# Writing down the order of TensorE, ScalarE and VectorE in the experts of a transformer block

## The chip, the cores and the metric

The kernel runs on one core of a Trainium2 chip. A core has a matrix engine (TensorE, PE in the rows), two elementwise engines (VectorE, DVE, and ScalarE, ACT), GpSimd (POOL) and SyncE (SP), which here issues most DMAs. Each engine takes its own instructions in the order in which they stand in its queue; semaphores hold one back until what it needs is there. The metric is the device time of one execution in microseconds, as the median of several runs.

## The reference

Two transformer layers on 256 tokens of width 1024. The second layer ends in a mixture of eight experts, and only that part is touched here:

```
logits = jnp.dot(t, w_router)                       # t: 256 x 1024
top_val, top_idx = lax.top_k(logits, 2)             # two experts for each token
gates = softmax(top_val) spread over the 8 experts
hid = silu(t @ e_w1) * (t @ e_w3)                   # e_w1, e_w3: 1024 x 3584 for each expert
y = sum over experts of (hid @ e_w2) * gate         # e_w2: 3584 x 1024
```

All inputs are float32; the weights of the experts alone are 352 MB.

## The kernel before

**Work of a chunk.** The tokens of an expert (at most 128) are gathered into one tile of 128 rows. Its 3584 hidden columns are taken in seven chunks of 512, so there are 56 chunks (`for e`, `for i`). For each chunk TensorE multiplies the tokens by w1 (into PSUM bank `b1`, 5 or 3) and by w3 (bank `b3`, 6 or 4). ScalarE takes silu of `b1` into the tile `nat` (L587), VectorE multiplies it by `b3` (L588). Four transposes on TensorE turn `nat` (`hid_t`, L599), and the turned tile is multiplied by w2 into banks 0 and 1, `y` (`down`). The down matmuls of a chunk are issued one chunk later (`pend`), behind the next chunk's w1 and w3.

**Splits.** float32 is reached by splitting every operand into a high and a low float32r part: ScalarE writes the high part `wh` (L154), VectorE the difference `wl` (L155). A product takes three matmuls (`mm3`): high by high (L176), high by `wl` (L177), low by `wh` (L178). One split covers 1024 columns of weights, two products of 512, so six matmuls. A chunk has twelve splits: four for w1, four for w3, four for w2. I number them 0 to 11. The pool `split` has four buffers of `wh` and four of `wl`, so ScalarE can split at most four splits ahead of TensorE. The turned hidden tile is split the same way (L182 high, L183 low, both named `ol_t`), as are the turned tokens of the next expert (`turn_x`, L876, split into `oh_t`).

**Weights.** SyncE loads 1 MB tiles (`raw`) into a ring of sixteen buffers in four pools; `load_ahead` issues a load as soon as, in program order, a buffer of the ring is used up.

**Order.** A scheduler places the instructions of each engine by its own estimate of when they are ready; `behind(a, b)` pins `a` behind `b` on one engine. In the experts before the change only a few places are pinned (the end of the routing, the gate product behind `added`).

**Sums at the end.** Seven experts send their result to DRAM (`store_y`); in the last expert `fetch` clears two ring buffers on GpSimd and gathers each token's rows into them, and `add_rows` adds them to `ht`, two VectorE instructions for each half of the tokens (L847).

Of the kernel before, what the change touches and what calls it, by code (L numbers as in the profile page):

```python
# [3 lines left out]

# [21 lines left out]
NE = 8  # L26
# [19 lines left out]
def block_kernel(ctx: ExitStack, tc: tile.TileContext, x, w_qkv, w_o, mixer_norm, ffn_norm,  # L46
# [91 lines left out]
    def stream(n, g=None, hold=(None, None), free=2):  # L138


        got = taken = 0
        while got < n:
            load_ahead()
            t = loaded[n_used[0]]
            _, nk, fn = jobs[n_used[0]]
            n_used[0] += 1
            k = min(nk, HALF // fn)
            for c0 in range(0, nk, k):
                wh = split.tile([P, HALF], F32R, name="wh")
# [24 lines left out]

    def mm3(ps, s, m, start, stop):
        i0 = nc.tensor.matmul(ps, s[0], m[0], start=start, stop=False)  # L176
        nc.tensor.matmul(ps, s[0], m[1], start=False, stop=False)  # L177
        i1 = nc.tensor.matmul(ps, s[1], m[0], start=False, stop=stop)  # L178
        return i0, i1

    def split_out(src, h, l):
        return (nc.scalar.activation(h, src, AF.Copy),  # L182
                nc.vector.tensor_sub(l, src, h.bitcast(F32)))  # L183
# [408 lines left out]
                                           op1=ALU.mult)  # L592
        return t

    def hid_t(t, n, ps, a, c, apart=True):
        k = n // P
        tv = t[:, :n].rearrange("p (f j) -> p j f" if apart else "p (j f) -> p j f", j=k)
        for j in range(k):
            nc.tensor.transpose(ps[:, j * P:(j + 1) * P], tv[:, j], ident)  # L599
        split_out(ps[:, :n], a[:, :n], c[:, :n])  # L600
        return [(a[:, j * P:(j + 1) * P], c[:, j * P:(j + 1) * P]) for j in range(k)]

    def down(ps, hT, j, w, start, stop):
        for half in range(2):
            mm3(ps[half], hT[j], tuple(a[:, half * FC:(half + 1) * FC] for a in w),
                start and j == 0, stop and j == len(hT) - 1)

    def dense_ffn(pool, hold, then):
        y = [[bank[0], bank[1]], [bank[2], bank[7]]]
# [2 lines left out]
        for i, (f0, n) in enumerate(fcs):  # L612
            if i == 0:
                for k in range(2):
                    ws = list(stream(NC, 2, hold[0]) if k == 0 else stream(NC, 2, hold[1], 0))
                    for b in range(NB):
                        for c, w in enumerate(ws):
# [2 lines left out]
                hid = [gate_mul(pool.tile([P, FC], F32, name="hid"), bank[3 + 2 * b],  # L620
                                bank[4 + 2 * b], n, rms[2][b]) for b in range(NB)]
                hT = [hid_t(hid[b], n, y[b][0], pool.tile([P, FC], F32R, name="hth"),
                            pool.tile([P, FC], F32R, name="htl"), False) for b in range(NB)]
            else:
                for k in range(2):
                    for c, w in enumerate(stream(NC, 2)):
# [215 lines left out]
                bounds_check=(NE - 1) * P - 1, oob_is_err=False)  # L842
        return t

    def add_rows(b, t):
        for k in range(2):
            i0 = nc.vector.scalar_tensor_tensor(ht[b], t[:, k * D:(k + 1) * D],  # L847
                                                ex[:, 1 + k, b:b + 1], ht[b], op0=ALU.mult,
                                                op1=ALU.add)
        return i0  # L850
# [5 lines left out]

    def store_y(e):
        t = ep.tile([P, D], F32, name="yr")
        nc.scalar.activation(t[:, :FC], y[0], AF.Copy)
        nc.vector.tensor_copy(t[:, FC:], y[1])  # L860
        nc.gpsimd.dma_start(ys_d[e * P:(e + 1) * P], t)


    def mark(e, b):
        return nc.vector.tensor_scalar(pe[:, b], iota, slot[:, b, e:e + 1], None, op0=ALU.is_equal)

    def take(i, bk):
        split_out(bank[bk], eh[:, 4 * i:4 * i + 4].rearrange("p c t -> p (c t)"),
                  el[:, 4 * i:4 * i + 4].rearrange("p c t -> p (c t)"))

    def turn_x(t, banks, later):

        for i in range(2):
            for c in range(4):
                cc = 4 * i + c
                behind((nc.tensor.transpose(bank[banks[i]][:, c * P:(c + 1) * P],  # L876
                                            t[:, cc * P:(cc + 1) * P], ident), later))
            take(i, banks[i])

    def gather(banks, later):  # L880

# [51 lines left out]
                i1 = nc.vector.tensor_add(ht[b][:, hs], ht[b][:, hs], ps)  # L933
        return i0, i1

    pend, done, added = None, None, None
    gather((3, 4), raws[2])
    k = 0
    most_v = None
# [2 lines left out]
    for e in range(NE):  # L942
        for i, (f0, n) in enumerate(ecs):
            b1, b3 = (5, 6) if k % 2 == 0 else (3, 4)
            k += 1
            for bk in (b1, b3):
# [12 lines left out]
            pend = (i, t, b1)  # L959
            if i == 0:  # L960
                if e:
                    store_y(e - 1)
                else:
                    gates()
                    send()
# [22 lines left out]
    hT = hid_t(pend[1], FC, bank[pend[2]], *(sp[0][:, i * FC:(i + 1) * FC] for i in range(2)))  # L988

    row = ep.tile([P, FC], F32, name="nat")  # L990
    one = sp[0][:, D:D + P]
# [142 lines left out]
```

## Time and profile before

| | |
|---|---|
| median of 3 runs | 1439.82 us (1438.69 to 1440.4) |
| profiled execution | 1438.46 us, of which 1436.8 us are the span from the first to the last instruction |
| TensorE busy | 1417.6 us, 99% |
| VectorE, ScalarE busy | 1170.2 us, 1010.3 us |
| mean granted TensorE clock | 0.996 of 2.4 GHz |
| DMA | 442 MB, 308 GB/s over the span |

The span is about 445 us of attention, dense layer and routing, then 966 us of experts (up to 1412 us), and 25 us of ending. Busy times are unions of intervals; a matmul's end is modelled, so TensorE reads as busy also where its matmuls start late. A stretch is therefore judged by how long the same work takes in it, not by its busy share.

### The profile page before, as it was taken

The page shows a single profiled execution, that of the slowest core. Times are in us where ns is not written, and L with a number is a line of the kernel's source. Part 1 is how long each engine was busy: PE and PEld are TensorE (multiplying, and loading weights), DVE is VectorE, ACT ScalarE, POOL GpSimd, SP SyncE. Part 2 cuts the span into 40 slices and gives each one's busy share as a digit, 9 for nine tenths or more (in the row PEclk, how much of TensorE's full clock was granted, in tenths as well). Part 3 has the DMA queues.
Part 4 walks back from the last instruction along what each step waited for, and adds up shares of the span by engine and source line. Part 5 has one row for each costly group of instructions (what it writes and reads, how often), then busy time and mean ns, then how long its engine had stood idle before and what let it go on. Part 6 is the DMA issues. An engine that isn't in the chain of part 4 may idle for free. (4 is left out here: it accounts for less than half of the span.)

```text
span 1436.8 us, 19637 instructions
## 1 busy us (share of the span) xinstructions
PE 1417.6 (99%) x7285; PEld 1176.7 (82%) x7285; DVE 1170.2 (81%) x1384; ACT 1010.3 (70%) x1282; POOL 45.3 (3%) x71
## 2 busy tenths in 40 slices
PE   9999999999999999999999999999999999999997
PEld 7877999988877888888888888878878887887775
DVE  6656766667667999999999988888888888898887
ACT  6656655546655778878878777777777777777765
POOL 1000000000001000000000000000000000000200
PEclk9999999999999999999999999999999999999998
DMA  9633865556566999999999999999999999999850
GB/s 353 236 117 108 303 196 186 186 173 228 180 246 218 402 401 388 385 373 373 388 392 362 391 362 373 366 381 368 354 389 372 357 380 380 358 374 369 320 189 32
DMA packets 172153, 442.11 MB, mean 308 GB/s; under 512 B 7299, under 2 KB 9395, under 8 KB 157972
## 3 DMA queue, kind: packets, MB, share of 16 engines
q1 hardware_dynamic: 166852, 422.61, 80.6%
q0 software_dynamic: 5136, 18.18, 3.5%
q8 instruction: 59, 0.97, 0.3%
q14 instruction: 42, 0.34, 0.1%
q10 hardware_dynamic: 64, 0.02, 0.0%
HBM read 430.00 MB, written 11.03 MB: 307 GB/s over the span
## 5 line engine op out<-in xcount | busy, mean ns | idle before, releaser
L155 DVE TENSOR_TENSOR wl<-raw,wh 128x1024 fp32r<-128x1024 f32 x710 | 834.4, 1220 | 112.9 <-ACT wh L154 106.0
L154 ACT ACTIVATE wh<-raw 128x1024 fp32r<-128x1024 f32 x710 | 725.6, 1057 | 133.9 <-PE bank L178 97.7
L177 PE MATMUL bank<-wl,oh_t 128*128 128x512 f32 x968 | 382.9, 396 | 2.9 <-DVE wl L155 2.0
L176 PE MATMUL bank<-wh,oh_t 128*128 128x512 f32 x968 | 375.5, 393 | 2.1 <-ACT wh L154 1.6
L178 PE MATMUL bank<-wh,oh_t 128*128 128x512 f32 x904 | 353.5, 391 | 0.1
L177 PEld LDWEIGHTS bank<-wl,oh_t 128*128 128x128 f32 x968 | 181.9, 188 | 60.0 <-DVE wl L155 18.9
L176 PEld LDWEIGHTS bank<-wh,oh_t 128*128 128x128 f32 x968 | 182.2, 188 | 41.4 <-ACT wh L154 1.8
L178 PEld LDWEIGHTS bank<-wh,oh_t 128*128 128x128 f32 x904 | 170.2, 188 | 34.1 <-DVE oh_t L183 0.8
L178 PE MATMUL bank<-wh,ol_t 128*128 128x512 f32 x504 | 194.6, 392 | 0.0
L162 ACT ACTIVATE wh<-raw,gcol 128x512 fp32r<-128x512 f32 (+1 forms) x192 | 123.8, 698 | 87.4 <-PE bank L318 56.3
L163 DVE SCALAR_TENSOR_TENSOR wl<-raw,gcol,wh 128x512 fp32r<-128x512 f32 (+1 forms) x192 | 131.1, 725 | 65.8 <-ACT wh L162 65.3
L177 PE MATMUL bank<-wl,ol_t 128*128 128x512 f32 x440 | 174.7, 397 | 0.4 <-DVE wl L155 0.4
L318 PE MATMUL bank<-x_h,wh 128*128 128x256 f32 x512 | 143.8, 282 | 0.0
L318 PE MATMUL bank<-x_h,wl 128*128 128x256 f32 x512 | 142.9, 280 | 0.0
L318 PE MATMUL bank<-x_l,wh 128*128 128x256 f32 x512 | 142.7, 279 | 0.0
L176 PE MATMUL bank<-wh,ol_t 128*128 128x512 f32 x440 | 137.1, 393 | 0.0
L178 PEld LDWEIGHTS bank<-wh,ol_t 128*128 128x128 f32 x504 | 94.4, 188 | 19.9 <-issue 1.1
L318 PEld LDWEIGHTS bank<-x_h,wh 128*128 128x128 f32 x512 | 95.9, 188 | 1.9 <-issue 1.1
L177 PEld LDWEIGHTS bank<-wl,ol_t 128*128 128x128 f32 x440 | 83.0, 189 | 16.4 <-DVE wl L155 0.6
L318 PEld LDWEIGHTS bank<-x_h,wl 128*128 128x128 f32 x512 | 96.1, 188 | 0.0
L318 PEld LDWEIGHTS bank<-x_l,wh 128*128 128x128 f32 x512 | 95.9, 187 | 0.2
L176 PEld LDWEIGHTS bank<-wh,ol_t 128*128 128x128 f32 x440 | 81.6, 188 | 16.8
(218 smaller groups left out, 1106.1 us busy)
## 6 DMA issues: line engine op xcount, KB each, us to landing
raw<-in_e_w_dram SPq DMA_DIRECT2D x335, 1024.0 KB, 7.3
raw<-in_w_dram SPq DMA_DIRECT2D x33, 1024.0 KB, 5.1
raw<-in_w_qkv_dram SPq DMA_DIRECT2D x22, 1024.0 KB, 5.7
raw<-in_w_o_dram SPq DMA_DIRECT2D x8, 1024.0 KB, 7.5
xs_d<-hn POOLq DMA_DIRECT2D x1, 4096.0 KB, 16.0
xr<-xs_d POOLq DMA_DIRECT2D x7, 512.0 KB, 7.5
ys_d<-yr POOLq DMA_DIRECT2D x7, 512.0 KB, 7.8
raw<-in_w_qkv_dram SPq DMA_DIRECT2D x4, 512.0 KB, 6.8
```

The lines of the kernel that those rows point to most:

```text
L154: i0 = nc.scalar.activation(wh[:, :m], src, AF.Copy)
L155: i1 = nc.vector.tensor_sub(wl[:, :m], src, wh[:, :m].bitcast(F32))
L162: i0 = nc.scalar.activation(wh[:, cs], src[:, cs], AF.Copy, scale=gc)
L163: i1 = nc.vector.scalar_tensor_tensor(wl[:, cs], src[:, cs], gc, wh[:, cs].bitcast(F32), op0=ALU.mult, op1=ALU.subtract)
L176: i0 = nc.tensor.matmul(ps, s[0], m[0], start=start, stop=False)
L177: nc.tensor.matmul(ps, s[0], m[1], start=False, stop=False)
L178: i1 = nc.tensor.matmul(ps, s[1], m[0], start=False, stop=stop)
L318: nc.tensor.matmul(to, w[a][:, ms], z[:, :, c], start=c + i + m % 2 == 0, stop=c == NC - 1 and m % 2 == 1 and i == 2, skip_group_check=True)
```

## The change

The instructions stay the same; only their order on the engines does not. Every matmul and transpose of the experts is now pinned behind the one before it in program order (`last`), so TensorE does w1, the four transposes, w3, then down, in every chunk. On ScalarE and VectorE each step that is not a weight split (`then`) stands behind the third split of the next weights, and the fourth split stands behind the step: the hidden tile's split and silu behind the third split of w3, the gate product and the next tokens' split behind the third split of w2, `store_y` behind the third split of the second chunk's w1. The fetch is issued one chunk earlier, and its four sums stand singly behind the third split of w1 in the last four chunks.

```diff
-    held, recent = [None, None], [None]
+    held, recent, lead = [None, None], [None, None], [None, None]
...
-                recent[0] = i0
+                recent[:] = i0, i1
...
+    def hid_t(t, n, ps, a, c, apart=True, after=None):
...
+            i0 = nc.tensor.transpose(ps[:, j * P:(j + 1) * P], tv[:, j], ident)
+            if after is not None:
+                behind((i0, after))
+                after = i0
+        h, l = split_out(ps[:, :n], a[:, :n], c[:, :n])
...
+    AHEAD, AHEAD_D = 6, 3
+
+    def ahead(ws, n):
+        return [next(ws) for _ in range(n)]
+
+    def then(act=None, dve=None):
+
+        for i, n in enumerate((act, dve)):
+            if n is not None:
+                behind((n, recent[i]), (n, lead[i]))
+                lead[i] = n
...
-                for c, w in enumerate(stream(NC, hold=held)):
-                    _, last = mm3(bank[bk], (eh[:, c], el[:, c]), w, c == 0, c == NC - 1)
-                if pend is not None and bk == b1:
-                    hT = hid_t(pend[1], FC, bank[pend[2]], *hts)
+                first = pend is None and bk == b1
+                ws = stream(NC, hold=held) if first else stream(NC, hold=lead, free=0)
+                got = [] if first else ahead(ws, AHEAD)
+                if bk == b1:
+                    if due is not None:
+                        then(*store_y(due))
+                        due = None
+                    if e == NE - 1 and i >= 3:
+                        then(dve=add_row((i - 3) // 2, (i - 3) % 2))
...
+                else:
+                    if pend is not None:
+                        hT, last, h, l = hid_t(pend[1], FC, bank[pend[2]], *hts, after=last)
+                        then(h, l)
+                    then(nc.scalar.activation(t[:, :n], bank[b1][:, :n], AF.Silu))
+                for c, w in enumerate(itertools.chain(got, ws)):
+                    i0, i1 = mm3(bank[bk], (eh[:, c], el[:, c]), w, c == 0, c == NC - 1)
+                    behind((i0, last))
+                    last = i1
+            if pend is not None:
+                ws = stream(4, hold=lead, free=0)
+                got = ahead(ws, AHEAD_D)
+            then(dve=nc.vector.tensor_mul(t[:, :n], t[:, :n], bank[b3][:, :n]))
             if i == len(ecs) - 1 and e + 1 < NE:
-                turn_x(xr, (2, 7), last)
-            t = gate_mul(ep.tile([P, FC], F32, name="nat"), bank[b1], bank[b3], n, after=added)
+                last = turn_x(xr, (2, 7), last)
             if pend is not None:
-                for j, w in enumerate(stream(4)):
-                    down(y, hT, j, w, pend[0] == 0, pend[0] == len(ecs) - 1)
+                for j, w in enumerate(itertools.chain(got, ws)):
+                    last = down(y, hT, j, w, pend[0] == 0, pend[0] == len(ecs) - 1, last)
...
-                elif i == 2:
+                elif i == 1:
                     came = [fetch(b) for b in range(NB)]
-                elif i in (4, 5):
-                    added = add_rows(i - 4, came[i - 4])
```

**Place 1: the hidden tile, middle experts.** On TensorE before, the four transposes (`nat` as input) that turn the hidden tile of the fourth expert's last chunk stand in the middle of the same chunk's down matmuls (banks 0 and 1), right after the product that makes `nat`:

```order
L177 MATMUL bank1_77<-wl_8574,ol_t_90 128x512
L178 MATMUL bank1_77<-wh_8573,ol_t_90 128x512
L599 MATMUL bank3_79<-ident_116,nat_8558 128x128 x4
L176 MATMUL bank0_76<-wh_8585,ol_t_90 128x512
L176 MATMUL bank1_77<-wh_8585,ol_t_90 128x512
L177 MATMUL bank0_76<-wl_8586,ol_t_90 128x512
```

The same transposes in the changed program, between the last w1 matmul (bank 5) and the first w3 matmul (bank 6) of the next chunk:

```order
L178 MATMUL bank5_81<-wl_8641,oh_t_89 128x512
L179 MATMUL bank5_81<-wh_8640,oh_t_89 128x512
L600 MATMUL bank3_79<-ident_116,nat_8452 128x128 x4
L177 MATMUL bank6_82<-wh_8652,oh_t_89 128x512
L178 MATMUL bank6_82<-wl_8653,oh_t_89 128x512
```

They moved back by 36 matmuls: twelve of down and the 24 of w1. On ScalarE in the same stretch before (`nat` is silu, `ol_t` the high part of the hidden tile):

```order
L154 ACTIVATE wh<-raw 128x1024 x8
L182 ACTIVATE ol_t<-bank_79 128x512
L154 ACTIVATE wh<-raw 128x1024 x4
L587 ACTIVATE nat<-bank_81 128x512
L154 ACTIVATE wh<-raw 128x1024 x8
```

and in the changed program:

```order
L155 ACTIVATE wh<-raw 128x1024 x12
L183 ACTIVATE ol_t<-bank_79 128x512
L988 ACTIVATE nat<-bank_81 128x512
L155 ACTIVATE wh<-raw 128x1024 x12
L183 ACTIVATE ol_t<-bank_81 128x512
```

The hidden tile's split moved four weight splits later and stands next to silu, once in twelve splits.

**Place 2: the first chunk of the first expert, VectorE.** Before (`gate` is the routing, `nat` the gate product of the first chunk):

```order
L155 TENSOR_TENSOR wl<-raw,wh 128x1024
L811 SCALAR_TENSOR_TENSOR gate<-isk,ex,gate 128x8
L155 TENSOR_TENSOR wl<-raw,wh 128x1024 x6
L588 TENSOR_TENSOR nat<-nat,bank_82 128x512
L155 TENSOR_TENSOR wl<-raw,wh 128x1024 x4
```

and in the changed program:

```order
L156 TENSOR_TENSOR wl<-raw,wh 128x1024
L817 SCALAR_TENSOR_TENSOR gate<-isk,ex,gate 128x8
L156 TENSOR_TENSOR wl<-raw,wh 128x1024 x3
L996 TENSOR_TENSOR nat<-nat,bank_82 128x512
L156 TENSOR_TENSOR wl<-raw,wh 128x1024 x7
```

The product moved ahead of three splits: it now stands directly behind split 7, the last of w3. On ScalarE the table load and silu of this chunk moved ahead of split 7.

**Place 3: the sums in the last expert, VectorE.** Before (`h_84` and `h_85` are the two halves of `ht`):

```order
L155 TENSOR_TENSOR wl<-raw,wh 128x1024 x9
L847 SCALAR_TENSOR_TENSOR h_84<-raw,ex,h_84 128x1024
L155 TENSOR_TENSOR wl<-raw,wh 128x1024
L847 SCALAR_TENSOR_TENSOR h_84<-raw,ex,h_84 128x1024
L588 TENSOR_TENSOR nat<-nat,bank_82 128x512
L847 SCALAR_TENSOR_TENSOR h_85<-raw,ex,h_85 128x1024
L183 TENSOR_TENSOR ol_t<-bank_81,ol_t 128x512
L155 TENSOR_TENSOR wl<-raw,wh 128x1024
L847 SCALAR_TENSOR_TENSOR h_85<-raw,ex,h_85 128x1024
```

and the second and third of the four sums in the changed program:

```order
L954 SCALAR_TENSOR_TENSOR h_84<-raw,ex,h_84 128x1024
L156 TENSOR_TENSOR wl<-raw,wh 128x1024 x4
L184 TENSOR_TENSOR ol_t<-bank_81,ol_t 128x512
L156 TENSOR_TENSOR wl<-raw,wh 128x1024 x4
L996 TENSOR_TENSOR nat<-nat,bank_80 128x512
L156 TENSOR_TENSOR wl<-raw,wh 128x1024 x4
L954 SCALAR_TENSOR_TENSOR h_85<-raw,ex,h_85 128x1024
```

The four sums stood within two weight splits of each other; now twelve splits, a hidden split and a product lie between one and the next.

## Rows read from the trace of the kernel before

**Rows 1.** Stretches: length, busy time of each engine, granted clock, DMA share, GB/s

```profile
559.85:678.62 118.77, 118.77 (x542) 98.80 (x540) 110.19 (x102) 96.01 (x101) 1.11 (x2) 1.00 1.01 378
...
797.39:918.45 121.06, 120.88 (x541) 97.96 (x540) 107.14 (x101) 91.92 (x100) 1.07 (x2) 1.00 1.01 373
918.45:1040.05 121.60, 121.42 (x541) 97.80 (x540) 107.64 (x102) 92.01 (x101) 1.07 (x2) 1.00 1.01 369
...
1283.25:1411.99 128.74, 124.66 (x548) 99.59 (x546) 113.73 (x107) 94.08 (x104) 9.85 (x8) 0.99 0.75 273
...
1400.06:1403.47 3.41, 3.41 (x9) 2.33 (x8) 3.41 (x4) 1.98 (x2) 0.00 (x0) 0.50 0.00 0
1403.47:1406.88 3.41, 3.41 (x16) 2.80 (x16) 3.25 (x4) 2.26 (x3) 0.00 (x0) 1.00 0.00 0
```

**Rows 2.** Waits of ScalarE, 821 to 1290 us: us in total, times, longest

```profile
ACT ol_t L182 <- PE bank L177: 43.6, 23, 2.0
```

**Rows 3.** Waits of TensorE's weight load, 821 to 1403 us

```profile
PEld bank L177 <- DVE wl L155: 19.3, 44, 1.1
```

**Rows 4.** Waits of SyncE's DMA queue, 470 to 1395 us

```profile
SPq L130 <- DVE wl L155: 772.9, 314, 10.0
```

**Rows 5.** Timeline (start, length, what, [idle before]), ScalarE and VectorE, fourth expert

```profile
907.25 0.60 ACT L182 ACTIVATE ol_t<-bank 128x512 fp32r<-128x512 f32 x1 [1.95 <-PE bank L177]
907.75 3.89 ACT L154 ACTIVATE wh<-raw 128x1024 fp32r<-128x1024 f32 x4
912.94 0.60 ACT L587 ACTIVATE nat<-bank 128x512 f32<-128x512 f32 x1 [1.30 <-PE bank L178]
...
902.52 4.62 DVE L155 TENSOR_TENSOR wl<-raw,wh 128x1024 fp32r<-128x1024 f32 x4
...
914.52 4.63 DVE L155 TENSOR_TENSOR wl<-raw,wh 128x1024 fp32r<-128x1024 f32 x4 [1.06 <-ACT wh L154]
```

**Rows 6.** Timeline of TensorE at the first of those four splits

```profile
915.46 0.39 PE L176 MATMUL bank<-wh,oh_t 128*128 128x512 f32 x1
915.80 0.50 PE L177 MATMUL bank<-wl,oh_t 128*128 128x512 f32 x1
```

**Rows 7.** Timeline of VectorE and TensorE around the sums, last expert

```profile
1393.89 1.28 DVE L847 SCALAR_TENSOR_TENSOR h<-raw,ex,h 128x1024 f32<-128x1024 f32 x1
1395.08 0.68 DVE L588 TENSOR_TENSOR nat<-nat,bank 128x512 f32<-128x512 f32 x1
1395.68 1.27 DVE L847 SCALAR_TENSOR_TENSOR h<-raw,ex,h 128x1024 f32<-128x1024 f32 x1
...
1395.82 0.74 PE L599 MATMUL bank<-ident,nat 128*128 128x128 f32 x4 [0.39 <-DVE nat L588]
1398.19 0.50 PE L176 MATMUL bank<-wh,oh_t 128*128 128x512 f32 x1 [1.63 <-ACT wh L154]
1399.45 0.50 PE L177 MATMUL bank<-wl,oh_t 128*128 128x512 f32 x1 [0.76 <-DVE wl L155]
```

**Rows 8.** Timeline of ScalarE and TensorE, end of the first chunk

```profile
460.15 1.28 ACT L587 ACT_TABLE_LOAD   x1
...
464.02 0.39 PE L178 MATMUL bank<-wh,oh_t 128*128 128x512 f32 x1
464.48 0.39 PE L177 MATMUL bank<-wl,oh_t 128*128 128x512 f32 x1
```

**Rows 9.** Timeline of TensorE around the last expert's extra transposes and products

```profile
1287.27 0.71 PE L176 MATMUL bank<-wh,ol_t 128*128 128x512 f32 x2
...
1288.40 0.48 PE L177 MATMUL bank<-wl,ol_t 128*128 128x512 f32 x1
```

**Rows 10.** Timeline of GpSimd's fetch, its line, and its DMAs to landing

```profile
1349.35 1.82 POOL L837 MEMSET raw<- 128x2048 f32 x1 [39.76 <-DVE wl L155]
...
L839 POOL DMA_INDIRECT raw<-ys_d,row_in x4: 1016/1158/1959, 1351.4 to 1357.5; - x4
...
DMA to landing us min/median/max: 4.6/4.9/7.2
```

More of the change, by code (lines that the diff above doesn't have):

```diff
@@ L1 @@
 import collections
+import itertools
 import math
@@ L593, in gate_mul @@
         return t
-    def hid_t(t, n, ps, a, c, apart=True):
+    def hid_t(t, n, ps, a, c, apart=True, after=None):
         k = n // P
@@ L598, in hid_t, with down @@
         for j in range(k):
[L599 to L603, printed above, removed]
+            i0 = nc.tensor.transpose(ps[:, j * P:(j + 1) * P], tv[:, j], ident)
[3 more added lines that the diff above has]
+        h, l = split_out(ps[:, :n], a[:, :n], c[:, :n])
+        return [(a[:, j * P:(j + 1) * P], c[:, j * P:(j + 1) * P]) for j in range(k)], i0, h, l
+    def down(ps, hT, j, w, start, stop, after=None):
         for half in range(2):
-            mm3(ps[half], hT[j], tuple(a[:, half * FC:(half + 1) * FC] for a in w),
-                start and j == 0, stop and j == len(hT) - 1)
+            i0, i1 = mm3(ps[half], hT[j], tuple(a[:, half * FC:(half + 1) * FC] for a in w),
+                         start and j == 0, stop and j == len(hT) - 1)
+            behind((i0, after))
+        return i1
     def dense_ffn(pool, hold, then):
@@ L622, in dense_ffn @@
                 hT = [hid_t(hid[b], n, y[b][0], pool.tile([P, FC], F32R, name="hth"),
-                            pool.tile([P, FC], F32R, name="htl"), False) for b in range(NB)]
+                            pool.tile([P, FC], F32R, name="htl"), False)[0] for b in range(NB)]
             else:
@@ L843, in fetch @@
         return t
[L845 to L850, printed above, removed]
     def load_x(e):
@@ L858, in store_y @@
         t = ep.tile([P, D], F32, name="yr")
-        nc.scalar.activation(t[:, :FC], y[0], AF.Copy)
-        nc.vector.tensor_copy(t[:, FC:], y[1])
+        i0 = nc.scalar.activation(t[:, :FC], y[0], AF.Copy)
+        i1 = nc.vector.tensor_copy(t[:, FC:], y[1])
         nc.gpsimd.dma_start(ys_d[e * P:(e + 1) * P], t)
+        return i0, i1
     def mark(e, b):
@@ L867, in take @@
     def take(i, bk):
-        split_out(bank[bk], eh[:, 4 * i:4 * i + 4].rearrange("p c t -> p (c t)"),
-                  el[:, 4 * i:4 * i + 4].rearrange("p c t -> p (c t)"))
+        return split_out(bank[bk], eh[:, 4 * i:4 * i + 4].rearrange("p c t -> p (c t)"),
+                         el[:, 4 * i:4 * i + 4].rearrange("p c t -> p (c t)"))
     def turn_x(t, banks, later):
@@ L875, in turn_x @@
                 cc = 4 * i + c
-                behind((nc.tensor.transpose(bank[banks[i]][:, c * P:(c + 1) * P],
-                                            t[:, cc * P:(cc + 1) * P], ident), later))
-            take(i, banks[i])
+                i0 = nc.tensor.transpose(bank[banks[i]][:, c * P:(c + 1) * P],
+                                         t[:, cc * P:(cc + 1) * P], ident)
+                behind((i0, later))
+                later = i0
+            then(*take(i, banks[i]))
+        return i0
     def gather(banks, later):
@@ L934, in scatter, with add_row @@
         return i0, i1
-    pend, done, added = None, None, None
+    AHEAD, AHEAD_D = 6, 3
[6 more added lines that the diff above has]
+                lead[i] = n
+    def add_row(b, k):
+        return nc.vector.scalar_tensor_tensor(ht[b], came[b][:, k * D:(k + 1) * D],
+                                              ex[:, 1 + k, b:b + 1], ht[b], op0=ALU.mult,
+                                              op1=ALU.add)
+    pend, done, last, due = None, None, None, None
     gather((3, 4), raws[2])
@@ L945, in block_kernel @@
             k += 1
+            t = ep.tile([P, FC], F32, name="nat")
             for bk in (b1, b3):
@@ L948, in block_kernel @@
                     held[:] = None, None
-                for c, w in enumerate(stream(NC, hold=held)):
-                    _, last = mm3(bank[bk], (eh[:, c], el[:, c]), w, c == 0, c == NC - 1)
-                if pend is not None and bk == b1:
-                    hT = hid_t(pend[1], FC, bank[pend[2]], *hts)
+                first = pend is None and bk == b1
[7 more added lines that the diff above has]
+                        then(dve=add_row((i - 3) // 2, (i - 3) % 2))
+                        if i == len(ecs) - 1:
+                            for m in range(i - 2, 4):
+                                then(dve=add_row(m // 2, m % 2))
+                else:
[11 more added lines that the diff above has]
+            then(dve=nc.vector.tensor_mul(t[:, :n], t[:, :n], bank[b3][:, :n]))
             if i == len(ecs) - 1 and e + 1 < NE:
-                turn_x(xr, (2, 7), last)
-            t = gate_mul(ep.tile([P, FC], F32, name="nat"), bank[b1], bank[b3], n, after=added)
+                last = turn_x(xr, (2, 7), last)
             if pend is not None:
-                for j, w in enumerate(stream(4)):
-                    down(y, hT, j, w, pend[0] == 0, pend[0] == len(ecs) - 1)
+                for j, w in enumerate(itertools.chain(got, ws)):
+                    last = down(y, hT, j, w, pend[0] == 0, pend[0] == len(ecs) - 1, last)
             pend = (i, t, b1)
@@ L961, in block_kernel @@
                 if e:
-                    store_y(e - 1)
+                    due = e - 1
                 else:
@@ L983, in block_kernel @@
                     done = slots(e)
-                elif i == 2:
+                elif i == 1:
                     came = [fetch(b) for b in range(NB)]
-                elif i in (4, 5):
-                    added = add_rows(i - 4, came[i - 4])
-    hT = hid_t(pend[1], FC, bank[pend[2]], *(sp[0][:, i * FC:(i + 1) * FC] for i in range(2)))
+    hT = hid_t(pend[1], FC, bank[pend[2]], *(sp[0][:, i * FC:(i + 1) * FC] for i in range(2)))[0]
     row = ep.tile([P, FC], F32, name="nat")
```

## The prediction, as it stood before the changed kernel ran

> **What bounds the kernel now.** I read the page first, then stretches, then waits, then the timeline. The page has TensorE busy 99% of the span, which looks like a kernel with nothing left in its order. The stretches say otherwise. Cut at the first transpose of each expert's turn, the second and third expert take 118.77 us each; the fourth takes 121.06, the fifth, sixth and seventh 121.60 each, and the last one, up to the end of its w3, 128.74 [rows 1]. The work is the same in the first six of these: seven chunks of 72 matmuls, 28 transposes of hidden tiles and 8 of tokens.
>
> Is 118.77 the pace of TensorE itself? At full clock fifteen matmuls start in 3.41 us, one every 0.2273 [rows 1], so 504 take 114.56, and 4.21 are left for 36 transposes, 0.117 each. Nothing is left for waiting: I take 118.77 as the floor, and a chunk as 72 × 0.2273 + 4 × 0.117 = 16.83.
>
> Where the slower experts lose time the waits show. From 821 to 1403 us TensorE's weight load stands 44 times before a matmul with `wl` for the split of VectorE, 19.3 us in all [rows 3]; before 821 us the same view is empty. VectorE in turn waits for ScalarE, and ScalarE for TensorE: 43.6 us, up to 2.0 at a time, at the hidden tile's high part [rows 2]. One chunk as an example: ScalarE stands 1.95 us before the hidden tile (place 1: only eight splits lie ahead of it, and its transposes are in the midst of down), and 1.30 before silu, for w1's last matmul. So its lead of four splits is used up, VectorE stands 1.06 [rows 5], and TensorE's matmul with that `wl` starts 0.34 after the one before it where 0.23 would do [rows 6]. The busy shares hide this, since a matmul counts as busy through its modelled end.
>
> The DMA is not the bound: 773 of the 925 us that I asked for SyncE's queue waits for VectorE to give a buffer back [rows 4], and at 118.77 the core moved 378 GB/s against 369 in the slower experts [rows 1], so it has carried the faster pace.
>
> **The change part by part.** No instruction is added or taken away; each term is a wait.
>
> *Experts two and three:* already at the floor; nothing.
>
> *Experts four to seven.* I go through one chunk of the new order with time 0 at the first w1 matmul. TensorE does w1 until 5.46, transposes until 5.93, w3 until 11.38, down until 16.83. ScalarE has a pitch of 0.95 per split and 1.05 to its end, VectorE (4.62 − 1.22)/3 = 1.13 and 1.22 [rows 5]; the product 0.60 and 0.68, a sum 1.19 and 1.28 [rows 7]; I give the hidden tile's low part the product's. The tightest split is 7, behind both steps on ScalarE. Split 6 is done early (its buffer is free when TensorE is past split 2, at 4.3, so it ends at 5.3). The hidden tile waits for the transposes, 6.1 to 6.7, silu 6.6 to 7.2, `wh` of split 7 7.1 to 8.15, `wl` 8.2 to 9.4. TensorE asks for it at 5.93 + 18 × 0.2273 + 0.23 = 10.25: 0.85 to spare. ScalarE does stand 0.8 before the transposes, but behind it only split 7 is queued soon enough to care. Split 11, behind the product, is split by 14.9 and wanted at 15.7, spare 0.8; the others have more. VectorE's whole chunk is 12 × 1.13 + 2 × 0.60 = 14.8 of 16.83, so delays are made up. Where an expert turns, two more splits of 0.60 on either engine are met by 0.9 more of transposes. So TensorE never waits and these four go to the floor: 121.06 + 3 × 121.60 − 4 × 118.77 = 10.78 saved.
>
> *Last expert.* Before, three of the four sums stood around the product and the hidden tile (place 3). The transposes came 0.39 late, the next `wh` 1.63, the next `wl` 0.76 [rows 7], and right after that the granted clock is 0.50, that is 1.2 GHz, for 3.41 us in which 9 matmuls stand instead of 15 or 16 [rows 1]. After, one sum is added to a chunk: 14.8 + 1.19 = 16.0 of 16.83 on VectorE; split 3 behind it keeps over 0.8. The expert has the floor's work, plus extra transposes and products between the second matmul of [rows 9] (start 1287.27 + 0.71 − 0.39) and 1288.40: 0.81 − 0.23 = 0.58. So 128.74 − 118.77 − 0.58 = 9.39 saved.
>
> The fetch must be in time for this. Each buffer is cleared for 1.82, two of its four DMAs are issued per buffer at 1.0 to 2.0, and they land in 4.6 to 7.2 [rows 10]. Counting buffers in turn, the two are free by the beginning of the third chunk; the first is filled after 2 × 1.82 + 2 × 1.2 + 7.2 = 13.2, and the first sum comes one chunk and some 1.3 later, at 18: 4.8 to spare. Two loads of the ring wait for such a buffer, with a chunk and more until they are used.
>
> *First chunk.* A loss. The product now stands directly behind split 7 (place 2) and must wait for w3's last matmul, start 464.02, end 464.41. It holds VectorE until 465.05, the next chunk's first `wl` ends at 466.28, and TensorE wants it at 464.48 [rows 8]: 1.82 lost. The table load of 1.28 [rows 8], now ahead of split 7, does not add to it: by the same pitches that split ends at 463.1, wanted at 463.12.
>
> *Start and ending:* the same order; nothing.
>
> Sum: −10.78 − 9.39 + 1.82 = −18.35. The profiled execution took 1438.46 (span 1436.8 and 1.66 around it), so 1420.1. The median of the runs lies 1.36 above it, so I say 1421.5.
>
> **A rule against it.** The rows show the clock at its lower level right after TensorE stood 0.39, 1.63 and 0.76 us within 4 us [rows 1, 7]. The first chunk's new wait is of that kind: 1.82, once. If it brings the lower level too, 3.41 us with 9 matmuls instead of 15 cost 6 × 0.2273 = 1.4, and the time is 1422.9. I give this 1 in 4. The Trainium skill, "TensorE: Matmul & The Clock Gate", Part 1, says that the throttled clock is the array's default and that activity lifts it; by that any wait of TensorE puts the clock at risk. Rows 1 agree at one place.
>
> **Rivals.** *The new order waits too, in every chunk* (the other side). ScalarE now has both its steps at one place, and if a semaphore or a PSUM read comes later than I took it, split 7 or 11 is late in all 55 chunks that have a hidden tile. For it: in the fourth chunk shown such waits did come from ScalarE. Against it: 0.8 to spare. If each chunk loses what the slower experts lose, (121.60 − 118.77)/7 = 0.40, the time is 1421.5 + 55 × 0.40 = 1443.5, slower than before; it decides at 18.35/55 = 0.33 per chunk, that is splits 1.15 later than I work them out. Chance 0.06. A milder case, half of it, gives 1432.5; chance 0.08.
>
> *The slower pace is not the order's*, but some contention that sets in at 800 us. Then only the last expert's sums and the first chunk count: 1421.5 + 10.78 = 1432.3. For it: nothing but the date; DMA and clock are alike in both [rows 1]. Chance 0.06.
>
> *The fetch lands late*: VectorE stands before the first sum with all splits behind it, 1 us for each us beyond 4.8, perhaps a stretch of lower clock: 1424 to 1430. Chance 0.03.
>
> *The change does nothing*: the places above exclude it. Chance 0.01.
>
> **How the numbers follow.** My forecast has the rest, 0.76, at 1418 to 1425: a tenth to either side of the saving, with the clock's 1.4. The range 1417 to 1432 takes in this case, the late fetch, and nearly half of the two at 1432: about 0.85, or 0.8 allowing for my bounds. A measurement of this kernel can tell 0.2%, 2.9 us. Faster by more than that holds for all but the other side, the idle change and an extreme of the milder case: 0.92; within it 0.03; slower 0.05.
>
> **What would show it.** Every expert from turn to turn at 118.8 with the weight load's wait for `wl` near zero; the last one near 119.4 up to the end of w3, with no lower clock in it; one wait of 1.8 of TensorE at the first gate product; ScalarE's wait for the hidden tile's transposes about 0.8 in every chunk. Wrong is the prediction if `wl` waits appear in the experts two and three, or a sum of the last expert waits for a DMA.

## The result and the profile after

The changed kernel takes 1420.99 us (median of 4 runs, 1420.87 to 1421.4) against 1439.82 before: a ratio of 0.9873, with a 95% interval of 0.9858 to 0.9887. The profiled execution has a span of 1419.6 us, 17.1 less than the one of before.

Stretches of the changed kernel, cut as in [rows 1] at the first transpose of an expert's turn: the second expert, the fifth, and the last one up to the end of its w3.

```profile
562.22:680.99 118.77, 118.77 (x541) 98.81 (x540) 109.34 (x102) 95.70 (x101) 1.10 (x2) 1.00 1.02 380
918.54:1037.31 118.77, 118.77 (x541) 98.80 (x540) 109.34 (x102) 95.71 (x101) 1.07 (x2) 1.00 1.01 380
1274.86:1394.31 119.45, 119.45 (x548) 99.48 (x547) 112.25 (x106) 95.97 (x103) 9.01 (x8) 1.00 0.78 293
```

All six whole experts now take 118.77 or 118.78. The last one has lost its stretch at the lower clock (1.00 in the first column behind the engines, as in the others).

The waits of ScalarE from 821 to 1290 us, the stretch of [rows 2], and those of VectorE and SyncE's queue from 470 to 1395:

```profile
ACT wh L155 <- PE bank L179: 59.0, 210, 0.3
ACT ol_t L183 <- PE bank L600: 21.6, 28, 0.8
...
DVE wl L156 <- ACT wh L155: 41.6, 56, 1.0
...
SPq L131 <- DVE wl L156: 754.0, 315, 7.2
```

The wait at the hidden tile is down from 2.0 to 0.8 and has another releaser: L600, the transposes, where before it was a matmul, L177. The wait at silu, in the same stretch before

```profile
ACT nat L587 <- PE bank L178: 36.1, 27, 1.5
```

is gone. The view that gave [rows 3], the weight load's waits, is empty from 470 to 1395 us. What ScalarE waits for now is mostly a free buffer (`wh` behind L179), 0.3 at a time: it is as far ahead as its four buffers allow.

In the first chunk the loss that was forecast is there. VectorE and TensorE around the first gate product (compare [rows 8]):

```profile
463.32 0.50 PE L178 MATMUL bank<-wl,oh_t 128*128 128x512 f32 x1
464.81 0.69 DVE L996 TENSOR_TENSOR nat<-nat,bank 128x512 f32<-128x512 f32 x1 [1.54 <-PE bank L179]
465.41 3.49 DVE L156 TENSOR_TENSOR wl<-raw,wh 128x1024 fp32r<-128x1024 f32 x3
466.69 0.50 PE L178 MATMUL bank<-wl,oh_t 128*128 128x512 f32 x1 [1.69 <-DVE wl L156]
```

VectorE stands 1.54 for w3's last matmul, with the next splits behind it, and TensorE then stands 1.69 for the first of those.

Where the 17.1 came from, by the marks of the two traces: up to the first turn +2.37, the six whole experts −10.76, the last expert −9.29 (128.74 to 119.45), what follows +0.54. The first and the last of these hold some chance: another execution of the same changed kernel, taken later, reaches its first turn at 563.38 us instead of 562.22, with every whole expert again at 118.77.

### The profile page after: what moved, and what is told of

It reads as the page before. It is cut to its first block, busy times and chain, and to the rows that moved or that the text cites. A ratio compares the mean times of both kernels' runs of the same rounds, so it can differ in the third digit from the quotient of the medians.

```text
span 1419.6 us, 19535 instructions
## 1 busy us (share of the span) xinstructions
PE 1402.5 (99%) x7285; PEld 1179.3 (83%) x7285; DVE 1173.6 (83%) x1384; ACT 1026.4 (72%) x1282; POOL 44.5 (3%) x71
## 5 line engine op out<-in xcount | busy, mean ns | idle before, releaser
L155 ACT ACTIVATE wh<-raw 128x1024 fp32r<-128x1024 f32 x710 | 740.2, 1062 | 181.2 <-PE bank L179 137.9
L177 PE MATMUL bank<-wh,oh_t 128*128 128x512 f32 x968 | 382.6, 396 | 0.5 <-ACT oh_t L183 0.5
L178 PE MATMUL bank<-wl,oh_t 128*128 128x512 f32 x968 | 376.7, 390 | 3.1 <-DVE wl L156 1.7
L179 PE MATMUL bank<-wh,oh_t 128*128 128x512 f32 x904 | 353.0, 391 | 0.9 <-DVE oh_t L184 0.8
L177 PEld LDWEIGHTS bank<-wh,oh_t 128*128 128x128 f32 x968 | 182.3, 188 | 37.0 <-ACT oh_t L183 1.2
L179 PEld LDWEIGHTS bank<-wh,oh_t 128*128 128x128 f32 x904 | 169.6, 188 | 38.0 <-DVE oh_t L184 1.6
L179 PE MATMUL bank<-wh,ol_t 128*128 128x512 f32 x504 | 194.0, 391 | 0.0
L178 PE MATMUL bank<-wl,ol_t 128*128 128x512 f32 x440 | 171.4, 390 | 0.0
L177 PE MATMUL bank<-wh,ol_t 128*128 128x512 f32 x440 | 136.1, 390 | 0.0
L179 PEld LDWEIGHTS bank<-wh,ol_t 128*128 128x128 f32 x504 | 94.3, 188 | 20.5 <-issue 1.1
L177 PEld LDWEIGHTS bank<-wh,ol_t 128*128 128x128 f32 x440 | 82.1, 188 | 16.7
```

## The experiments

All are timed against the kernel before on the same chip; its median was 1440.4, 1440.11 and 1439.14 us in the three sets. "Split 6" is the third split of w3, as numbered above.

**The slower order, everywhere.** Before the change the two steps of ScalarE drift between the second expert and the fifth. Counted through its whole order, one round of ScalarE is:

```
before, experts 2 and 3:  silu | 8 9 10 11 0 1 2 | hidden tile | 3 4 5 6 7 | silu
before, experts 4 to 7:   silu | 6 7 8 9 10 11 0 1 | hidden tile | 2 3 4 5 | silu
after, every expert:      hidden tile, silu | 7 8 9 10 11 0 1 2 3 4 5 6 | hidden tile, silu
```

(Place 1 above counts from silu to silu. That shows how far the hidden tile's split moves against silu, and not that silu itself moves: in the fourth to the seventh expert from behind split 5 to behind split 6.) So before, silu moved from behind split 7 to behind split 5, and the hidden tile from behind split 2 to behind split 1. Three kernels take the second line for every chunk, with the transposes after twelve of down's matmuls. The first has just that, with the product behind split 9, and `store_y` and the sums of the last expert behind split 1; its core:

```diff
-                got = [] if first else ahead(ws, AHEAD)
+                got = [] if first else ahead(ws, 4 if bk == b1 else 4)
                 if bk == b1:
...
+                    if pend is not None:
+                        hT = cut(pend)                # hidden tile's split, behind split 1
...
-                got = ahead(ws, AHEAD_D)
+                got = ahead(ws, 2)
...
+                    if j == 1 and not (e == NE - 1 and i == len(ecs) - 1):
+                        last = turn(t, b1, last)      # the four transposes, within down
```

> The changed kernel with the order of the slower experts of before written into every chunk: transposes after twelve of down's matmuls, the hidden tile's split behind the second split of w1, silu behind the second of w3, the product behind the second of w2. Theory (the order is the cause): each of the experts two to seven takes 121.6 us instead of 118.8, the six chunks of the first lose 0.4 each, the last one 2 to 3, so 1421 + 17 + 2.4 + 2.5 = 1443 us, with about one late wl in each chunk. Rival (something that sets in at 800 us): the second and third expert stay at 118.8.

Measured: 1445.8 us (1443.9 to 1448.14), ratio 1.0034 (1.0023 to 1.0046). All six whole experts take 121.10 to 121.13, the second as well as the seventh. So it is the order and not the date. The order written here costs 121.10 − 118.77 = 2.33 of the 2.83 us that the slower experts of before lose; the other 0.5 was not looked into.

The other two take the two long waits of ScalarE apart. The view of before shows what ended the wait of 1.95 in [rows 5]. TensorE in that chunk:

```profile
904.50 0.63 PE L599 MATMUL bank<-ident,nat 128*128 128x128 f32 x4
...
906.82 0.40 PE L177 MATMUL bank<-wl,ol_t 128*128 128x512 f32 x1
907.05 0.39 PE L178 MATMUL bank<-wh,ol_t 128*128 128x512 f32 x1
```

The transposes were over at 905.13. The hidden tile's high part was written from 907.25, 0.03 behind the end of L177, the last matmul that read the old one. The wait was for the tile's only buffer. One kernel therefore gives it a second, from tiles that lie unused until the ending:

```diff
-        a, c = hts
+        a, c = ys if pend[0] % 2 else hts
```

> The same order as in the kernel with the slower order everywhere, but the hidden tile alternates between two buffers. Theory A (ScalarE's wait of 1.95 us at the hidden tile's high part uses up its lead; the wait ends with the last matmul that reads the old tile, 2.1 us after the transposes): the wait falls below 0.2 and the experts go to 118.8, 1421 us. Theory B (the wait of 1.30 at silu is what counts; its two steps stand too early among the splits, and the split behind silu starts at the same time with or without the first wait): the experts stay at 121.6, about 1443 us.

The other moves silu alone, from behind split 5 to behind split 7:

```diff
-                got = [] if first else ahead(ws, 4 if bk == b1 else 4)
+                got = [] if first else ahead(ws, 4 if bk == b1 else 8)
```

> The slower order everywhere with one hidden tile, and only silu moved on ScalarE, from behind the second split of w3 to behind the fourth. Theory B (silu's place): the wait at silu goes, the wait at the hidden tile (1.95) stays, and the experts are at 118.8, 1421 us. Theory A (the hidden tile's wait): the experts stay near 121.6, about 1443 us.

Measured: 1443.25 us with two buffers (ratio 1.0021, 1.0011 to 1.003), 1427.44 with silu moved (0.9913, 0.9896 to 0.9929). ScalarE's longest waits from 562 to 1270 us and one expert, first of the slower order, then with two buffers, then with silu moved:

```profile
ACT ol_t L183 <- PE bank L178: 64.3, 35, 1.9
ACT nat L1000 <- PE bank L179: 52.2, 40, 1.3
...
687.85:808.95 121.10, 121.10 (x541) 97.80 (x540) 107.68 (x102) 91.94 (x101) 1.07 (x2) 1.00 1.01 371
```

```profile
ACT nat L1000 <- PE bank L179: 64.1, 40, 1.7
...
688.14:809.53 121.39, 121.39 (x541) 98.19 (x540) 107.25 (x102) 94.00 (x101) 1.07 (x2) 1.00 1.00 372
```

```profile
ACT ol_t L183 <- PE bank L178: 66.2, 36, 1.9
...
681.35:800.58 119.23, 119.23 (x541) 98.32 (x540) 107.70 (x101) 93.52 (x101) 1.07 (x2) 1.00 1.02 381
```

Theory B holds in the main. The larger wait, at the hidden tile, can be taken away whole (second fence: no such row) and the experts get no faster, 121.39. It can stay whole (third fence) and they come to 119.23. What costs is silu: it stands two splits too early, and the splits behind it start too late whatever happened before. Of the 0.46 that the third kernel still lacks to 118.77, 0.30 lies in one chunk, the one behind the expert's turn (17.14 us from one hidden tile's transposes to the next, 16.84 in the changed kernel; the other chunks have 16.87). Another 3.1 us of its distance to the changed kernel lie behind the last turn. Neither was followed further.

**Which engine's order is needed.** One kernel has the pins on ScalarE and VectorE without those on TensorE (the pins inside `hid_t` and `down` go too), one those on TensorE alone. A piece of each:

```diff
-                    behind((i0, last))        # TensorE left to itself: e_no_pe
...
-            if n is not None:
-                behind((n, recent[i]), (n, lead[i]))
-                lead[i] = n
+            pass                              # ScalarE and VectorE left: e_pe_only
```

> The changed kernel with its order of ScalarE and VectorE, and without the pins on TensorE, which then does the transposes behind 18 of down's 24 matmuls and the first two of down ahead of the last five or six of w3. Theory (the places of the steps on ScalarE and VectorE decide): experts at 118.8, in all 1421 us, give or take 1. Rival (TensorE's order is needed): a wait in every chunk of 0.2 or more, so 1432 us or more.

> The changed kernel with its order of TensorE, and without the pins that hold the steps of ScalarE and VectorE behind the third split. Its own order then puts the hidden tile and silu behind the fourth split of w3, and the four sums of the last expert within four splits of each other. Theory (the steps of ScalarE must not stand early; the sums must stand singly): experts two to seven at 118.8 and no wait in the first chunk (1.7 less than the changed kernel), the last expert 2 to 4 longer, in all 1421 to 1424 us. Rival (all pins are needed): experts over 121, 1436 us or more.

Measured: 1421.36 us without TensorE's pins (0.9872, 0.9855 to 0.9888), every whole expert at 118.77. With TensorE's alone 1445.51 (1.0038, 1.0025 to 1.0051), which is slower than before the change. The second expectation failed, and its stretches say where: the third expert, then the fifth.

```profile
679.24:798.01 118.77, 118.77 (x541) 98.81 (x540) 111.38 (x101) 96.63 (x101) 1.07 (x2) 1.00 1.02 384
921.02:1044.70 123.68, 120.96 (x541) 98.25 (x540) 107.70 (x102) 94.33 (x101) 1.07 (x2) 1.00 0.99 365
```

ScalarE in each of the two, at the hidden tile:

```profile
708.05 1.06 ACT L155 ACTIVATE wh<-raw 128x1024 fp32r<-128x1024 f32 x1 [0.30 <-PE bank L179]
709.02 0.58 ACT L183 ACTIVATE ol_t<-bank 128x512 fp32r<-128x512 f32 x1
...
1000.45 1.06 ACT L155 ACTIVATE wh<-raw 128x1024 fp32r<-128x1024 f32 x1 [0.30 <-PE bank L179]
1003.64 0.60 ACT L183 ACTIVATE ol_t<-bank 128x512 fp32r<-128x512 f32 x1 [2.13 <-PE bank L600]
```

I had read "twelve splits, hidden tile, silu" in every chunk of its order and taken it for one place. It isn't: at the fourth expert's turn two rounds hold eleven splits, and the steps slide from behind split 7 to behind split 5. The rows look alike ever after; only the count from the start tells them apart.

**One split earlier, with everything else pinned.** If that reading is right, the changed kernel with its steps behind the second split instead of the third must come to the same pace:

```diff
-    AHEAD, AHEAD_D = 6, 3
+    AHEAD, AHEAD_D = 4, 3
```

> The changed kernel with the steps at w1 and w3 behind the second split of the next weights instead of the third; the transposes stay between w1 and w3. Theory (a step that stands too early holds the splits behind it): the third split of w3 starts at 7.1 as the fourth did, its low part is there at 9.4, TensorE asks at 8.9, so 0.5 late and 0.2 to be back at the pace, 0.5 to 0.7 for each of 55 chunks: 1449 to 1460 us, slower than before the change. Rival (the place by one split doesn't matter, only the order of TensorE does): 1421 us.

Measured: 1461.79 us (1.0147, 1.0130 to 1.0163), 1.8 us above the range that was expected. Whole experts take 123.63 to 123.70, as in the kernel above, that is 0.70 more in a chunk. One split makes the difference between 1.3% faster and 1.5% slower than before.

**How much time is to spare.** The sum had 0.85 us at the tightest split, 7. Silu done two and four times in a row uses it up:

```diff
+                    if pend is not None:
+                        for _ in range(1):        # 3 in the other kernel
+                            then(nc.scalar.activation(t[:, :n], bank[b1][:, :n], AF.Silu))
```

> The changed kernel with silu done twice in a row in each of the 55 chunks that have a hidden tile, 0.48 us more on ScalarE each time. The sum of the prediction has 0.85 to spare at the tightest split: 0.37 is left, no wait, 1421.0 us, within 0.5. Rival (the spare time is less than 0.5): a wait in every chunk, 0.2 or more each, 1432 us or more.

> Silu four times in a row in each of those 55 chunks, 1.44 us more on ScalarE. By the spare 0.85 the split behind it comes 0.59 late, and TensorE needs some 0.2 to be back at its pace: 0.6 to 0.8 for each chunk, 33 to 44 us in all, 1454 to 1465 us. Rival (ScalarE has more room, since it is busy for 96 of 119 us): below 1430 us.

Measured: 1424.99 (0.9893, 0.9876 to 0.9909) and 1490.57 us (1.0347, 1.0330 to 1.0364). Both expected times, 1421.0 and 1454 to 1465, were missed. Four silus in one chunk, ScalarE, then TensorE (a repeat is the form with a line of its own, L991):

```profile
857.36 0.60 ACT L183 ACTIVATE ol_t<-bank 128x512 fp32r<-128x512 f32 x1 [0.77 <-PE bank L600]
857.85 0.59 ACT L988 ACTIVATE nat<-bank 128x512 f32<-128x512 f32 x1
858.48 1.86 ACT L991 ACTIVATE nat<-bank 128x512 f32<-128x512 f32 x3
860.23 4.91 ACT L155 ACTIVATE wh<-raw 128x1024 fp32r<-128x1024 f32 x5
...
861.34 0.50 PE L177 MATMUL bank<-wh,oh_t 128*128 128x512 f32 x1
862.60 0.50 PE L178 MATMUL bank<-wl,oh_t 128*128 128x512 f32 x1 [0.76 <-DVE wl L156]
```

My price of a repeat, 0.48, was too low. A silu that writes what the one before it wrote starts 0.63 behind it, so three of them put the splits back by 1.90: from the hidden tile's start to the next split it is 2.87 here, and 0.97 in the changed kernel. TensorE's matmul comes 862.60 − 861.34 − 0.23 = 1.03 late, and 1.90 − 1.03 = 0.87 was to spare: the 0.85 of the prediction. The chunk pays 1.25, 0.2 more than the wait.

One repeat leaves 0.85 − 0.63 = 0.22. No wait is listed, and still an expert takes 119.20 instead of 118.77. Eleven matmuls start 0.232 apart on average instead of 0.227. The repeat itself does not slow them: in the chunk at 728 us it runs at 729.31, and the slower pace begins with split 7's first matmul, at 732.12. So the last quarter of a microsecond of the spare time isn't free.

**The sums.** All four behind the same split of the sixth chunk:

```diff
-                    if e == NE - 1 and i >= 3:
-                        then(dve=add_row((i - 3) // 2, (i - 3) % 2))
...
+                    if e == NE - 1 and i == 5:
+                        for m in range(4):
+                            then(dve=add_row(m // 2, m % 2))
```

> The changed kernel with its four sums of the last expert all behind the third split of w1 of the sixth chunk, instead of one in each of four chunks. One sum leaves 0.8 us to spare at the next split; three more of 1.19 make it 2.8 late: one wait of TensorE of 2.8, 1423.8 us. If the granted clock then falls as it did in the last expert of before, 1.4 more: 1425.2 us. Rival (VectorE's lead takes them up, singly or not): 1421 us.

> The changed kernel itself once more, beside the next kernels on the same chip: 1421.0 us, within 0.5.

Measured: 1426.06 us, against 1422.68 of the changed kernel in the same set (ratios to before 0.9904, 0.9889 to 0.9920, and 0.9883, 0.9867 to 0.9898). The second is 1.7 above the 1421.0 that was expected: the same kernel differs that much from one set to another. VectorE and TensorE at the sums:

```profile
1369.55 5.12 DVE L954 SCALAR_TENSOR_TENSOR h<-raw,ex,h 128x1024 f32<-128x1024 f32 x4
...
1375.85 0.50 PE L178 MATMUL bank<-wl,oh_t 128*128 128x512 f32 x1 [2.91 <-DVE wl L156]
...
1370.00:1380.00 10.00, 7.09 (x33) 5.61 (x33) 9.88 (x10) 5.40 (x7) 0.00 (x0) 1.00 0.19 61
```

One wait of 2.9 as worked out, and the granted clock stays at 1.00, its upper level. So bunching alone can cost some 3 us; how that compares with the 9.3 of the last expert is said below.

**The first chunk.** Its product is put behind the third split of the next w1, as everywhere else:

```diff
...
+            else:
+                early = stream(NC, hold=lead, free=0)
+                early = early, ahead(early, AHEAD)
             then(dve=nc.vector.tensor_mul(t[:, :n], t[:, :n], bank[b3][:, :n]))
```

> The changed kernel, but in the first chunk of the first expert the product stands behind the third split of the next w1, as in all other chunks, and not directly behind the last split of w3. Theory: TensorE's wait of 1.69 us for that product goes, 1419.3 us. Rival (the wait hides something that comes next, a load or the transposes, which then wait instead): 1420.5 to 1421 us.

Measured: 1420.0 us (1419.17 to 1420.77), ratio to before 0.9865 (0.985 to 0.988). It is the fastest kernel of the set. From the first w1 matmul to the first transposes of a hidden tile it takes 17.76 us, the changed kernel 19.77 in the same set: 2.0 less, the wait of 1.69 and what TensorE needs to be back at its pace. That 2.0 is what this change is worth. The rest of the 2.7 between the medians is not its doing: in the two traces, 0.9 us lie ahead of the first w1 matmul and 0.4 in the ending, where the programs do the same.

On top of that, silu's table was to be loaded earlier:

```diff
-        nc.scalar.activation(ex[:, 0], ex[:, 0], AF.Exp)
+        i0 = nc.scalar.activation(ex[:, 0], ex[:, 0], AF.Exp)
+        warm = small.tile([P, NB], F32, name="warm")
+        behind((nc.scalar.activation(warm, ex[:, 0], AF.Silu), i0))
```

> The same, and the table of silu is loaded by a small silu right behind the routing's exponential, where ScalarE waits for buffers, instead of at the first silu. Theory: also the 0.34 us that TensorE waits there for the last split of w3 goes, 1419.0 us; silu starts 1.28 earlier. Rival (the load makes the splits of w1 late): a new wait at 456 to 459 us, 1419.5 us or more.

Measured: 1445.62 us (1.0042, 1.0028 to 1.0056), 25 slower, and neither theory foresaw it. No wait of TensorE is new. Every whole expert takes 121.84. TensorE in the dense layer, 140 us before the added instruction runs, first in this kernel, then in the one without it:

```profile
312.12 0.39 PE L177 MATMUL bank<-wh,hth 128*128 128x512 f32 x1
312.35 0.40 PE L178 MATMUL bank<-wl,hth 128*128 128x512 f32 x1
312.59 0.39 PE L179 MATMUL bank<-wh,htl 128*128 128x512 f32 x1
312.82 0.40 PE L177 MATMUL bank<-wh,hth 128*128 128x512 f32 x1
...
313.52 0.39 PE L177 MATMUL bank<-wh,hth 128*128 128x512 f32 x1
```

```profile
312.31 0.39 PE L177 MATMUL bank<-wh,hth 128*128 128x512 f32 x1
312.53 0.39 PE L178 MATMUL bank<-wl,hth 128*128 128x512 f32 x1
312.76 0.39 PE L179 MATMUL bank<-wh,htl 128*128 128x512 f32 x1
312.99 0.39 PE L177 MATMUL bank<-wh,hth 128*128 128x512 f32 x1
...
313.67 0.61 PE L177 MATMUL bank<-wh,hth 128*128 128x512 f32 x2
```

Six matmuls take 1.40 in the one and 1.36 in the other, 0.233 and 0.227 each, at the same clock. On TensorE and VectorE the two programs have the same order, and on ScalarE they differ only by the added instruction and the place of the table load. What differs at 312 us is where tiles lie: in the built program the new tile moves many of those allocated behind it by 64 bytes in each partition, among them the matmuls' stationary tiles (`oh_t`, `ol_t`, `hth`, `htl`), while `wh` and `wl` stay. That the address does it, and which tile's, was not tried with a kernel of its own and stays open.

One thing on record points to the stationary tile. `x_h` and `x_l`, the turned tokens of the layers ahead of the experts, lie at the same place in both programs. Where they are the stationary operand of matmuls of 512 columns, the faster kernel has the slower pace as well:

```profile
16.09 0.39 PE L177 MATMUL bank<-wh,x_h 128*128 128x512 f32 x1
...
17.49 0.39 PE L177 MATMUL bank<-wh,x_h 128*128 128x512 f32 x1
```

Six take 1.40, 0.233 each, at a granted clock of 1.00. In the built programs `x_h` and `x_l` begin 96 bytes behind a multiple of 128. So do the moved stationary tiles in the slower program; in the faster one they begin 32 behind. These are two places only, and no rule follows from them.

## Why the prediction was right, and where not

**The time.** 1421.5 was forecast, 1420.99 measured; for the profiled execution 1420.1 and 1421.4. That the medians agree to 0.5 is in part luck: the sum of the terms was 1.2 too large a saving, and the 1.36 added between the profiled execution and the median did not come again (1421.4 is the highest of the four runs). By terms:

| term | forecast | measured |
|---|---|---|
| experts four to seven | −10.78 | −10.76 |
| last expert, to the end of w3 | −9.39 | −9.29 |
| up to the first turn | +1.82 | +2.37 |
| ending | 0 | +0.54 |
| sum | −18.35 | −17.14 |

**Experts four to seven.** The size was right because the floor of 118.77 was read from two experts of the same trace. The reason was half wrong. The prediction named both waits of ScalarE, the 1.95 at the hidden tile first, and said that with both its lead is used up; it laid the 1.95 to the transposes in the midst of down. The runs show that this wait was for the old tile's last reader, that taking it away gains nothing (121.39), and that moving silu alone brings the experts to 119.23. The order of TensorE, which the change pins with the most lines, isn't needed for the time once ScalarE's and VectorE's is written down.

**The rival on the other side.** "The new order waits in every chunk" was to decide at splits 1.15 us later than worked out. It did not come, as the spare 0.85 was there within 0.02. But it lay nearer than that figure says: steps one split earlier give 1461.79, and beyond the spare time a chunk pays 0.2 on top of the wait, which the prediction had left out.

**Last expert.** The size was right because it, too, was a difference to the floor. The sums come singly, and the fetch is in time. The second DMA of the fetch, the time to landing of all four, and the four sums in the changed kernel:

```profile
1319.31 1.01 POOL L845 DMA_INDIRECT raw<-ys_d,row_in  x1 [0.31 <-issue]
...
DMA to landing us min/median/max: 6.5/7.0/7.8
...
L954 DVE SCALAR_TENSOR_TENSOR h<-raw,ex,h x4: 1278/1279/1279, 1333.5 to 1384.0; 128x1024 f32<-128x1024 f32 x4
```

Two DMAs fill the first buffer, by 1319.3 + 7.8 = 1327.1 at the latest; the first sum starts 6.4 later, where 4.8 was worked out. Of the 9.29, the three waits of [rows 7] are 2.78, about what the four sums cost when bunched, and the lower clock is 1.4 by the prediction's estimate. If this expert paid for its order what the slower ones pay, 2.83, some 2.3 are left. The kernel before was not taken apart here any further.

**First chunk.** The wait was forecast at 1.82 (its own figures, 466.28 − 464.48, give 1.80) and the matmul came 466.69 − 464.61 − 0.23 = 1.85 late (the matmul before it started at 464.61); being back at its pace costs TensorE another 0.2, which the prediction left out. And "the table load does not add to it" failed: split 7 was worked out to end 0.02 before it is wanted. It came just too late (the 463.32 row above), for some 0.2 more. A margin of 0.02 was no margin. By the tenth matmul of the first w1 the two traces are 0.11 apart (455.41 before, 455.52 after), so 2.26 of the 2.37 come from this chunk.

**Ending.** "The same order; nothing" missed half a microsecond: at the branch in the ending TensorE's sequencer stood 1.37 us, 0.84 in the same place before. The changed kernel in its later execution stood 1.25. Before, after, and after once more:

```profile
1423.77 0.47 PE L177 MATMUL bank<-wl,oh_t 128*128 128x512 f32 x1 [0.84 <-PEq L1063]
```

```profile
1406.64 0.47 PE L178 MATMUL bank<-wl,oh_t 128*128 128x512 f32 x1 [1.37 <-PEq L1104]
```

```profile
1407.70 0.47 PE L178 MATMUL bank<-wl,oh_t 128*128 128x512 f32 x1 [1.25 <-PEq L1104]
```

The kernel with the first chunk's product moved, whose ending is the same, stood 0.82. That the change made this term is therefore not shown.

**The clock.** The 1 in 4 for a stretch at 1.2 GHz did not come: behind the wait of 1.69 the clock stayed at 1.00, and behind that of 2.91 as well. The rule that I drew from three waits within 4 us [rows 1, 7] does not hold either. The trace of before has a second stretch at the lower level, in the routing, that I had overlooked. There TensorE stood 0.35, 0.68 and 1.19 us, before the matmuls at 443.06, 445.32 and 447.47. The changed kernel has the same three waits, and its clock stays up. The same stretch, before and after:

```profile
447.74:451.16 3.42, 3.42 (x19) 3.30 (x18) 3.21 (x13) 0.00 (x0) 0.16 (x1) 0.50 0.02 6
```

```profile
447.74:451.16 3.42, 2.94 (x24) 2.73 (x25) 3.32 (x16) 0.00 (x0) 0.16 (x1) 1.00 0.02 5
```

So the same waits are followed by the lower level in one execution and not in another. The fall in the last expert may be such a case, and its 1.4 us then belong to the profiled execution and not to the order: from run to run of the kernel before, the mean granted clock goes from 0.993 to 0.998. The Trainium skill, "TensorE: Matmul & The Clock Gate", Part 1, says that the throttled clock is the default and that activity lifts it. My step from there, that any wait puts the clock at risk, was not borne out by the single waits here.

## What to carry to other kernels

When an engine's steps stand between splits that another engine is waiting for, the count of splits ahead of each step decides, and the longest wait need not be the one that costs: ask which instruction behind it is wanted next, and when. Count a step's place from the start of the order, since a repeating pattern looks the same when it has slipped by one. And keep a quarter of a microsecond more to spare than the sum says, since a matmul whose operand comes just in time already slows the ones behind it.

## What was not expected of the hardware

A late operand costs TensorE more than its lateness. In the changed kernel's first chunk a `wl` came less than 0.1 late; that matmul and the next start 0.30 and 0.35 apart, and the following ones 0.23 to 0.24, instead of 0.227. With 0.22 us still to spare (silu twice) an expert loses 0.43 without any listed wait.

A tile of 8 bytes in each partition, allocated ahead of others, goes with 0.233 instead of 0.227 for the matmuls of 512 columns whose stationary tile it moved, 25 us in all. Those on `x_h` and `x_l`, which it did not move, have 0.233 in both programs. The many matmuls of 256 columns of the layers ahead of the experts keep 0.118, but neither of their operands was moved. The Trainium skill, "SBUF — State Buffer", section "Operand start alignment", says of start addresses what is legal, and that its runs timed nothing. These runs show a difference in time; a kernel that moves one stationary tile alone would show its cause.

The lower clock does not follow from TensorE's waits alone: 0.35, 0.68 and 1.19 us were followed by 3.4 us at 1.2 GHz in one execution and by 2.4 GHz in another.
